# The blocks of w_out summed and split beside the last head's attention, and fetched as parts

## The chip, the cores and the metric

The kernel runs on one core of one Trainium2 chip. The metric is the time of one execution in microseconds (us), taken on the device; a kernel's time is the median of its runs. Times in profiles count from the start of the profiled execution's span, from its first to its last instruction.

## The reference

One layer of an encoder trunk, with SEQ = D_MODEL = 1024, in float32. What the change touches are the lines of the output projection; the rest is told as far as it stands around it.

```python
h = rmsnorm(x, norm_mix[l])
proj = h @ w_in[l]
q, k, v, r, lr_f, lr_b, u, g_a, g_b = jnp.split(proj, split_points, axis=-1)
...
o = o_fwd + o_bwd                       # gated linear attention, 4 heads, both directions
o = o * lax.rsqrt(jnp.mean(o * o, axis=-1, keepdims=True) + EPS)
o = (o * jax.nn.silu(r.astype(jnp.float32))).astype(x.dtype)
y_a = o @ w_branch_gla[l]
...
merged = jax.nn.sigmoid(g_a) * y_a + jax.nn.sigmoid(g_b) * y_b
x = x + merged @ w_out[l]
h2 = rmsnorm(x, norm_ffn[l])
gate, up = jnp.split(h2 @ w_ffn_in[l], 2, axis=-1)
x = x + (jax.nn.silu(gate) * up) @ w_ffn_out[l]
return rmsnorm(x, norm_final)
```

## The kernel before

**Products.** A float32 factor is split into a rounded part (`hi`, type float32r, a cast on ACT at L200) and the rest (`lo`, a subtraction at L201 on DVE or POOL); each product of two blocks is three matmuls, hi x hi, hi x lo and lo x hi (`mm3`, L279). The large products are also cut into 2 x 2 blocks and made by seven products of sums of blocks in place of eight (numbers p = 1 to 7 in the names). So sums of blocks of a weight are needed: for w_out those with p = 4, 5, 6 and 7; p = 1, 2, 3 take a block as it is. An output has its columns interleaved in two halves; `sorted_` reads a row sorted (elements two apart), `halves` reads it in natural order as two halves.

**Stages**, in order of time: norm, q, k, v and the attention of four heads, to about 310 us; the projection of R in six steps j = 0 to 5 of two halves, to about 342 (`feature_major`; what j = 0 to 2 give is put by, and from j = 3 on each half ends in two calls of `gated`, one for j - 3 that was put by and one for j: SiLU on ACT, four transposes `tp<-ident,ol` of the attention's output on PE, a product on DVE, L1206); the gates (gate n = 0 to 10), to about 554; the branch project with w_branch (14 pieces in the order p = 1, 2, 6, 5, 7, 3, 4, two each), to 629; the merged project with w_out (p = 1, 4, 6, 7, 5, 2, 3), to 709; then the FFN and the last norm.

**What sets the order.** The schedule is written out: every engine executes its instructions, and SP issues all DMAs, in the order in which the program emits them. `pump` (L161) is called after each product with the time that this product takes in units of a matmul of 512 columns; it lets work run that stands beside: `pending` (splits of the next weights), `side` (attention of the next head) and `aside`. `aside` holds jobs that `prepare_beside` (L735) put there; `beside` (L695) does one per `every` units: issue stores that are `put` steps old, subtract for the part `lo`, cast for the part `hi`, then the job's own sum. `finish_beside` (L738) runs what is left of them at once. In the projection of R this is called at the first half from j = 3 on at which no attention is left in `side`.

**The sums of w_out** (`output_jobs`, L629): for each of four rows k of blocks, two loads of 512 KB (`wsum`, L608), and four subtractions on POOL, each stored into `t_wo`, 256 KB. They are queued at gate n = 1 and run from 353 to 415 us. A merged piece with p = 4, 5, 6 or 7 loads two such sums (`wraw`, L1312) and splits them with two casts on ACT (L200) and two subtractions on POOL (L201).

**The last head's attention** runs from `side` beside the projections at about 260 to 310 us. Its state is a chain: a step on DVE (`st`, L924), two scalings on ACT (`sb`, `so`, L928 and L932), a step on DVE again. `raw` are the tiles of weights for the next projection and `ol` the attention outputs of a head that come back from HBM (`load_o`, L1040), one head at each of j = 2, 3 and 4. The transposes for j read the head j // 2: those of j = 4 read the third head, loaded at j = 4, ahead of its first half.

**Merging** (`merge`, L1625): the branch's block (1,1), made while p = 7 ends, adds a gate product `yb` on POOL (L1639) whose rows are read with `sorted_`.

Of the kernel before, what the change touches and what calls it, by code (L numbers as in the profile page):

```python
# [17 lines left out]
P = 128  # L18
# [35 lines left out]
def kernel(  # L54
# [537 lines left out]


    s_out = {p: dram.tile([P, 4, HALF], F32, name=f"s_out{p}") for p in (3, 5, 6, 7)}
    t_wo = {p: dram.tile([P, 4, HALF], F32, name=f"t_wo{p}") for p in (4, 5, 6, 7)}
    READY = 2
    f_order = [f for q in range(PAIRS) for f in (q, q + PAIRS)]
    u_out = [{p: dram.tile([P, 2, HALF], F32, name=f"u_out{n}_{p}") for p in range(1, 8)} for n in range(READY)]
# [31 lines left out]
    def output_jobs(k):  # L630
        (b11, b12, b21, b22), loads = rows_of(w_out, k)
        yield from loads
        for dst, a, b, p in ((b11, b12, b11, 5), (b12, b22, b12, 7), (b22, b22, b11, 6), (b21, b21, b22, 4)):
            yield partial(psub, dst, a, b), None, t_wo[p][:, k, :]

    def unit_jobs(n):
        raw = [slot(F32, (KT, P), "fraw")[:, :, :] for _ in range(2)]
# [54 lines left out]
            return [t2(dtype=F32R, s=s)[:, :] for s in ("uph", "upl")]  # L692
        return [slot(F32R, s=s)[:, :, :] for s in ("trh", "trl")]

    def beside(jobs, every, put, lag):  # L695

        casts, differ = [None] * lag, None
        puts = [[] for _ in range(put)]
        while True:
            job = next(jobs, None)  # L700
            if not any((job, *casts, differ, *puts)):
                return
            if put:
                for pair in puts.pop(0):
                    nc.sync.dma_start(*pair)
            puts.append([])
            if differ:
                src, (hi, lo), dst = differ
                nc.vector.tensor_tensor(lo, src, as_f32(hi), op=ALU.subtract)
                if len(src.shape) == 2:  # L710
                    puts[-1] += [(dst[:, i, :], as_f32(t)) for i, t in enumerate((hi, lo))]
                else:
                    right.setdefault(dst, []).append((hi, lo))
            differ, cast = None, casts.pop(0)
            if cast:
                src, dst = cast
                parts = parts_for(src)
                nc.scalar.copy(parts[0], src)
                differ = src, parts, dst
            casts.append(None)  # L720
            if job:
                op, src, dst = job
                if op:
                    op()
                if src is not None:
                    casts[-1] = src, dst
                elif dst is not None:

                    puts[-1].append((dst, op.args[0]))
            if not put:  # L730
                for pair in puts.pop():
                    nc.sync.dma_start(*pair)
            yield every

    def prepare_beside(jobs, every, put=PUT, lag=1):  # L735
        aside.append([beside(chain(*jobs), every, put, lag), every])

    def finish_beside():  # L738
        while aside:
# [329 lines left out]
    for h in range(HEADS):  # L1069
        if h:  # L1070
            project_qk(h, h == 2)
        else:
            first_qk()
            begin(attention(0))
        if h < HEADS - 1:
            begin(attention(h + 1))
        if h == 0:
            for ts in ((7,), (6,), (5, 4)):
                pair_products(ts)
            prepare_beside(map(branch_jobs, range(4)), 4.2)  # L1080
        if h == 2:
            value_weights.pop().products()

    class Unit:
# [206 lines left out]
    def line_load():  # L1291
        if len(loads) < len(line):
            loads.append(line[len(loads)][0]())

    def line_sums():
        if len(begun_sums) < len(line):
            begun_sums.append(line[len(begun_sums)][1]())

    def line_make():
        n = len(made)  # L1300
        if n < len(line):
            while len(loads) <= n:
                line_load()
            if len(begun_sums) <= n:
                while len(begun_sums) <= n:
                    line_sums()
                settle()
            made.append(line[n][2](loads[n]))

    def weight_load(src):  # L1310
        raw = slot(s="wraw")
        nc.sync.dma_start(raw[:, :, :], src)  # L1312
        return raw

    def weight_split(raw):
        parts = []
# [66 lines left out]
    def merged_piece(p, c):  # L1383
        def load():
            if p in WEIGHT_B:
                i, j = WEIGHT_B[p]
                return weight_load(chunk(w_out, i, j, c))
            return weight_load(t_wo[p][:, 2 * c : 2 * c + 2, :])

        def sums():  # L1390
            def block(i, j):
                return merged[i, j][c][:, :, :]

            if p == 6:
# [11 lines left out]
        return load, sums, make  # L1406

    line += [merged_piece(p, c) for p in MERGED for c in range(2)]

# [53 lines left out]
    class Gates:  # L1463
# [7 lines left out]
        def row(self, i):  # L1471
            while len(self.rows) <= i:
                self.rows.append(slot(s="ga"))
            return self.rows[i]

        def run(self, p):
            while len(right.get(p, ())) < 2:
                next(aside[0][0])
            ps = bank_of(self, p)
            product(self.unit, p, ps, right)  # L1480
            ps = ps[:, :]
            if self.kind in "ur":
                ps = sorted_(ps)
            finish_late()

            def row(i, half):
                t = self.row(i)[:, half, :]
                return halves(t) if self.kind in "ur" else t

            part = {1: (0, 0), 6: (0, 1), 5: (1, 1)}.get(p)  # L1490
            if part:
                nc.scalar.copy(row(*part), ps)  # L1492
                return
            i, half = {2: (0, 0), 3: (0, 1), 4: (1, 0), 7: (1, 1)}[p]
            done = row(i, half)
            if p != 4:
                add(done, ps, done)
# [16 lines left out]
        def pooling(self, i, half):  # L1514
            yb = bank(ps_g, "yb")
            mm3(
                yb[:, :], tuple(t[:, i * P : (i + 1) * P] for t in wpool[self.at]),
                tuple(t[:, half, :] for t in pools[self.at]), True, True,
            )
            j, row = 2 * self.at + i, self.row(i)[:, half, :]  # L1520
            late.append(partial(
                nc.vector.scalar_tensor_tensor, row, yb[:, :], g_pool[:, j : j + 1], row, op0=ALU.mult, op1=ALU.mult
            ))

        def store(self, i):
# [58 lines left out]
    def project(base, products, collect, before, amid=None, first=FIRST, up=UP, pools_of=lambda p: U_BANKS if p == 1 else X_BANKS):  # L1584
        banks = {}
        for at, p in enumerate(products):
# [4 lines left out]
            for c in range(2):  # L1591
# [36 lines left out]
    def merge(i, j, m, ps, s):  # L1628
# [6 lines left out]
        if (i, j) == (1, 1):  # L1635
            dst = halves(dst)
            add(dst, sorted_(ps), sorted_(s))
            nc.vector.tensor_tensor(dst, dst, sorted_(sa), op=ALU.mult)
            padd(dst, dst, sorted_(yb))  # L1639
            return  # L1640
        if s is not None:
            add(ps, ps, s)
# [513 lines left out]
```

## Time and profile before

| | |
|---|---|
| median of 3 runs | 1325.27 us (1325.08 to 1325.62) |
| the profiled execution's own time | 1323.53 us |
| its span | 1321.8 us |
| attention and projections, 0 to 310 us | PE busy 303.82 us |
| projection of R, 310 to 342 | PE busy 32.00 of 32.00 us |
| gates, 342 to 554 | PE busy 211.32 of 212.00 us |
| branch project, 554.57 to 629.45 | PE busy 73.11 of 74.88 us |
| merged project, 629.67 to 709 | PE busy 77.05 of 79.33 us |
| FFN and end, 709 to 1321.8 | PE busy 604.08 of 612.80 us |

The rows by stage are busy times of TensorE (PE) in stretches of the span. PEld is its loading of weights, DVE is VectorE, ACT is ScalarE, POOL is GpSimd, SP is SyncE, which issues DMAs. A row of the timeline gives start and duration in us, engine, line, operation, output<-inputs, shapes and count, and in brackets the idle time ahead and what ended it. A row of a tile gives the durations in ns (least/median/most) and the first and last start. A row of a wait gives the total, the number of times and the longest. A row of windows gives for each engine busy time and instructions, then the granted clock of PE (1.00 is full), the DMA engines' share and GB/s.

### The profile page before, as it was taken

What the parts mean: (1) busy time and instruction counts of PE and PEld (TensorE: products, weight loads), DVE (VectorE), ACT (ScalarE), POOL (GpSimd) and SP (SyncE); (2) the same over time, 40 slices, a digit from 0 to 9 for tenths busy, and PEclk for the clock granted to TensorE, in tenths of its full rate; (3) what the DMA queues carried; (4) which work ended last, traced back from release to release, by engine and by line L of the source; (5) the groups of instructions that cost most, each with busy time, mean ns of one, the idle gap of its engine ahead of it and who ended that gap; (6) DMA issues with size and microseconds to landing.
All of it is one profiled execution on the core that took longest, in us unless ns stands there. A gap on an engine that the chain in (4) does not pass through costs nothing. (4 is left out here: it accounts for less than half of the span.)

```text
span 1321.8 us, 17901 instructions
## 1 busy us (share of the span) xinstructions
PE 1302.2 (99%) x6310; PEld 1138.0 (86%) x6310; DVE 838.3 (63%) x1034; ACT 645.3 (49%) x1177; POOL 769.0 (58%) x557
## 2 busy tenths in 40 slices
PE   9999999999999999999999999999999999999998
PEld 7888888899888888888888888888888888888886
DVE  6975556554735876778884856566666657354375
ACT  7366766665534545554347633333333334454353
POOL 3332734132598657669675286777766778465454
PEclk9999999999999999999999999999999999999999
DMA  7231623134778678996516355555444457995562
GB/s 236 104 104 42 198 75 117 59 101 128 239 247 283 195 223 303 380 409 212 185 65 240 127 189 186 183 183 173 155 142 159 150 160 257 382 349 201 182 223 80
DMA packets 167835, 251.97 MB, mean 191 GB/s; under 512 B 11161, under 2 KB 94145, under 8 KB 167745
## 3 DMA queue, kind: packets, MB, share of 16 engines
q1 hardware_dynamic: 167600, 250.57, 55.8%
q8 instruction: 49, 0.80, 0.3%
q14 instruction: 42, 0.34, 0.1%
q10 hardware_dynamic: 144, 0.26, 0.1%
HBM read 168.74 MB, written 82.05 MB: 190 GB/s over the span
## 5 line engine op out<-in xcount | busy, mean ns | idle before, releaser
L201 POOL TENSOR_TENSOR wl<-fs,wh 128x512 fp32r<-128x512 f32 x124 | 190.7, 1543 | 138.8 <-ACT wh L200 80.9
L279 PE MATMUL ps<-gh,wh 128*128 128x512 f32 x616 | 234.4, 381 | 0.5 <-DVE sums L1880 0.3
L279 PE MATMUL ps<-gl,wh 128*128 128x512 f32 x616 | 233.6, 379 | 0.7 <-DVE gl L1713 0.7
L279 PE MATMUL ps<-gh,wl 128*128 128x512 f32 x616 | 233.5, 379 | 0.0
L201 POOL TENSOR_TENSOR wl<-fraw,wh 128x512 fp32r<-128x512 f32 x93 | 131.1, 1410 | 58.0 <-ACT wh L200 52.8
L201 POOL TENSOR_TENSOR ol<-gor,oh 128x1024 fp32r<-128x1024 f32 (+1 forms) x42 | 103.2, 2462 | 76.0 <-ACT oh L200 63.1
L279 PE MATMUL ps<-hh,wh 128*128 128x512 f32 x356 | 141.1, 396 | 0.7 <-ACT ga L1492 0.7
L279 PE MATMUL ps<-hh,wl 128*128 128x512 f32 x356 | 134.9, 379 | 0.0
L279 PE MATMUL ps<-hl,wh 128*128 128x512 f32 x356 | 134.9, 379 | 0.0
L279 PEld LDWEIGHTS ps<-gh,wh 128*128 128x128 f32 x616 | 116.5, 189 | 17.9 <-DVE sums L1880 0.7
L279 PEld LDWEIGHTS ps<-gl,wh 128*128 128x128 f32 x616 | 116.4, 189 | 17.4 <-DVE gl L1713 1.1
L279 PEld LDWEIGHTS ps<-gh,wl 128*128 128x128 f32 x616 | 116.4, 189 | 16.5
L279 PE MATMUL ps<-oh,oh 128*128 128x512 f32 x308 | 116.8, 379 | 0.2 <-DVE g L1886 0.2
L279 PE MATMUL ps<-ol,oh 128*128 128x512 f32 x308 | 116.7, 379 | 0.0
L279 PE MATMUL ps<-oh,ol 128*128 128x512 f32 x308 | 116.7, 379 | 0.0
L201 POOL TENSOR_TENSOR wl<-wraw,wh 128x512 fp32r<-128x512 f32 x56 | 91.4, 1663 | 38.3 <-ACT wh L200 36.2
L201 POOL TENSOR_TENSOR wl<-raw,wh 128x512 fp32r<-128x512 f32 x34 | 47.0, 1392 | 103.2 <-ACT wh L200 70.3
L201 DVE TENSOR_TENSOR ol<-wor,oh 128x1024 fp32r<-128x1024 f32 (+1 forms) x42 | 66.6, 1601 | 62.6 <-ACT oh L200 55.1
L200 ACT CAST wh<-fs 128x512 fp32r<-128x512 f32 x124 | 75.8, 612 | 25.7 <-DVE fs L1104 23.8
L279 PEld LDWEIGHTS ps<-hh,wl 128*128 128x128 f32 x356 | 67.3, 189 | 9.6
L279 PEld LDWEIGHTS ps<-hh,wh 128*128 128x128 f32 x356 | 67.4, 189 | 9.3 <-ACT ga L1492 1.1
L279 PEld LDWEIGHTS ps<-hl,wh 128*128 128x128 f32 x356 | 67.4, 189 | 8.4
(281 smaller groups left out, 3059.4 us busy)
## 6 DMA issues: line engine op xcount, KB each, us to landing
fraw<-in_w_ffn_in_dram SPq DMA_DIRECT2D x44, 512.0 KB, 5.9
gor<-g_out SPq DMA_DIRECT2D x35, 512.0 KB, 5.7
fraw<-in_w_in_dram SPq DMA_DIRECT2D x22, 512.0 KB, 6.1
g_out<-s SPq DMA_DIRECT2D x44, 256.0 KB, 2.4
wor<-t_out SPq DMA_DIRECT2D x20, 512.0 KB, 4.2
raw<-in_w_in_dram SPq DMA_DIRECT2D x36, 256.0 KB, 5.2
g_out<-g SPq DMA_DIRECT2D x33, 256.0 KB, 2.6
x<-in_x_dram SPq DMA_DIRECT2D x16, 512.0 KB, 5.2
```

The lines of the kernel that those rows point to most:

```text
L200: nc.scalar.copy(hi, src)
L201: eng.tensor_tensor(lo, src, as_f32(hi), op=ALU.subtract)
L279: nc.tensor.matmul(ps.rearrange("p (c a) -> p c a", a=2), a, b.rearrange("p (a c) -> p c a", a=2), **flags)
```

## The change

Three parts. (1) `output_jobs` moves from gate n = 1 (`every` 2.8, `put` 3, `lag` 1) to the third head's turn in the loop over heads (h = 2, `every` 3.3, `put` 1, `lag` 2, first job after 32 units), beside the last head's attention. The sums are now also split there, by a cast on ACT and a subtraction on DVE for each of 16, and `t_wo` holds both parts, so that a store has 512 KB. (2) The merged pieces with p = 4, 5, 6, 7 fetch both parts straight into the tiles `wh` and `wl`: 32 loads of 256 KB in place of 8 loads of 512 KB, 16 casts on ACT and 16 subtractions on POOL. (3) The gate product that the branch's block (1,1) adds (`yb`, gates of kind "b", half 0, `at` >= 2) is written with its rows sorted, so that `merge` reads them in natural order.

```diff
-    t_wo = {p: dram.tile([P, 4, HALF], F32, name=f"t_wo{p}") for p in (4, 5, 6, 7)}
+    t_wo = {p: dram.tile([P, 4, 2, HALF], F32, name=f"t_wo{p}") for p in (4, 5, 6, 7)}
...
-            yield partial(psub, dst, a, b), None, t_wo[p][:, k, :]
+            yield partial(psub, dst, a, b), dst, t_wo[p][:, k]
...
-    def beside(jobs, every, put, lag):
+    def slot_parts(src):
+        w = slot(F32R, s="wop")
+        return w[:, 0, :], w[:, 1, :], w[:, :, :]
+
+    def beside(jobs, every, put, lag, home):
...
-                src, (hi, lo), dst = differ
+                src, (hi, lo, *both), dst = differ
                 nc.vector.tensor_tensor(lo, src, as_f32(hi), op=ALU.subtract)
-                if len(src.shape) == 2:
+                if both:
+                    puts[-1].append((dst, as_f32(both[0])))
+                elif len(src.shape) == 2:
...
-                parts = parts_for(src)
+                parts = home(src)
...
-    def prepare_beside(jobs, every, put=PUT, lag=1):
-        aside.append([beside(chain(*jobs), every, put, lag), every])
+    def prepare_beside(jobs, every, put=PUT, lag=1, home=parts_for, delay=None):
+        aside.append([beside(chain(*jobs), every, put, lag, home), every if delay is None else delay])
...
         if h == 2:
+            prepare_beside(map(output_jobs, range(4)), 3.3, 1, 2, slot_parts, 32)
             value_weights.pop().products()
...
+    fetched = {}
+
+    def line_fetch():
+        n = len(made)
+        if n < len(line) and n not in fetched and line[n][3:]:
+            fetched[n] = line[n][3]()
...
-            made.append(line[n][2](loads[n]))
+            line_fetch()
+            made.append(line[n][2](fetched.get(n) or loads[n]))
...
+    def weight_parts(src):
+        parts = [wts.tile([P, HALF], F32R, tag=s, name=name(s))[:, :] for s in ("wh", "wl")]
+        for i, t in enumerate(parts):
+            nc.sync.dma_start(as_f32(t), src[:, i, :])
+        return parts
...
-            return weight_load(t_wo[p][:, 2 * c : 2 * c + 2, :])
...
-            return data_split(a, 3.5 if p == 3 else 2), weight_split(raw)
+            return data_split(a, 3.5 if p == 3 else 2), weight_split(raw) if p in WEIGHT_B else raw
...
+        def fetch():
+            return [weight_parts(t_wo[p][:, 2 * c + k]) for k in range(2)]
...
+        def sorts(self, half):
+            return self.kind in "ur" or self.kind == "b" and half == 0 and self.at >= 2
...
-            if self.kind in "ur":
-                ps = sorted_(ps)
...
+            if self.sorts(half):
+                ps = sorted_(ps)
...
-            j, row = 2 * self.at + i, self.row(i)[:, half, :]
+            j, row, yb = 2 * self.at + i, self.row(i)[:, half, :], yb[:, :]
+            if self.sorts(half):
+                row, yb = halves(row), sorted_(yb)
...
-        if n == 1:
-            prepare_beside(map(output_jobs, range(4)), 2.8)
...
                 line_make()
+                line_fetch()
                 line_sums()
...
-            padd(dst, dst, sorted_(yb))
+            padd(dst, dst, halves(yb))
```

How the instructions stand on their engines shows what moves. First SP, in the kernel before, in the projection of R at j = 3 to 5. `raw` are weights of R (the first pair of j = 4, the second of j = 5), `hs` a sum for the gates, `ol` the third head's output, which `gated` reads at j = 4.

```order
L208 DMA raw_3155<-in_w_in_dram 128x4x128
L208 DMA raw_3157<-in_w_in_dram 128x4x128
L684 DMA hs_3349<-f_out_563 128x1024
L1044 DMA ol_3376<-o_out_567 128x1024
L1044 DMA ol_3377<-o_out_567 128x1024
L208 DMA raw_3380<-in_w_in_dram 128x4x128
L208 DMA raw_3382<-in_w_in_dram 128x4x128
```

The same place on SP in the changed kernel; `wop` is a sum of w_out in its two parts, `wsum` a row of w_out's blocks, and the stores to `t_wo` are of 512 KB.

```order
L709 DMA t_wo_544<-wop_3387 128x1024
L608 DMA wsum_3394<-in_w_out_dram 128x1024
L608 DMA wsum_3395<-in_w_out_dram 128x1024
L709 DMA t_wo_546<-wop_3391 128x1024
L709 DMA t_wo_545<-wop_3398 128x1024
L709 DMA t_wo_543<-wop_3404 128x1024
L709 DMA t_wo_544<-wop_3411 128x1024
L709 DMA t_wo_546<-wop_3415 128x1024
L709 DMA t_wo_545<-wop_3420 128x1024
L709 DMA t_wo_543<-wop_3424 128x1024
L684 DMA hs_3445<-f_out_563 128x1024
L1050 DMA ol_3472<-o_out_567 128x1024
```

Between the weights of j = 4 and `hs` now stand sixteen more DMAs, of which the last ten are shown: the stores wait for the parts, and the two loads of the last row stand behind a store.

DVE at the same place, in the kernel before: the products of `gated` in j = 3's first half (two rows), in its second half (two rows), and the first of j = 4.

```order
L1206 SCALAR_TENSOR_TENSOR o_3320<-tp_3315,cols,sr_3313 128x512
L1206 SCALAR_TENSOR_TENSOR o_3330<-tp_3325,cols,sr_3323 128x512
L1206 SCALAR_TENSOR_TENSOR o_3321<-tp_3362,cols,sr_3360 128x512
L1206 SCALAR_TENSOR_TENSOR o_3331<-tp_3370,cols,sr_3368 128x512
L1206 SCALAR_TENSOR_TENSOR o_3320<-tp_3430,cols,sr_3428 128x512
```

And in the changed kernel, from the second product of j = 3's first half on:

```order
L1213 SCALAR_TENSOR_TENSOR o_3375<-tp_3370,cols,sr_3368 128x512
L713 TENSOR_TENSOR wop_3333<-wsum_2957,wop_3333 128x512
L713 TENSOR_TENSOR wop_3380<-wsum_2957,wop_3380 128x512
L713 TENSOR_TENSOR wop_3387<-wsum_3329,wop_3387 128x512
L713 TENSOR_TENSOR wop_3391<-wsum_3329,wop_3391 128x512
L713 TENSOR_TENSOR wop_3398<-wsum_3330,wop_3398 128x512
L713 TENSOR_TENSOR wop_3404<-wsum_3330,wop_3404 128x512
L713 TENSOR_TENSOR wop_3411<-wsum_3394,wop_3411 128x512
L713 TENSOR_TENSOR wop_3415<-wsum_3394,wop_3415 128x512
L713 TENSOR_TENSOR wop_3420<-wsum_3395,wop_3420 128x512
L713 TENSOR_TENSOR wop_3424<-wsum_3395,wop_3424 128x512
L1213 SCALAR_TENSOR_TENSOR o_3366<-tp_3458,cols,sr_3456 128x512
```

Ten subtractions stand in a row between the two halves of j = 3.

The third place is SP beside the last head's attention. In the kernel before (`o_out` are stores of a head's output, the first `raw` are weights of R for j = 2, the second for j = 3):

```order
L574 DMA o_out_567<-o_2494 128x1024
L208 DMA raw_2832<-in_w_in_dram 128x4x128
L208 DMA raw_2834<-in_w_in_dram 128x4x128
L1044 DMA ol_2961<-o_out_565 128x1024
L1044 DMA ol_2962<-o_out_565 128x1024
L208 DMA raw_2965<-in_w_in_dram 128x4x128
```

In the changed kernel:

```order
L608 DMA wsum_2785<-in_w_out_dram 128x1024
L608 DMA wsum_2786<-in_w_out_dram 128x1024
L208 DMA raw_2836<-in_w_in_dram 128x4x128
L208 DMA raw_2838<-in_w_in_dram 128x4x128
L709 DMA t_wo_544<-wop_2894 128x1024
L608 DMA wsum_2956<-in_w_out_dram 128x1024
L608 DMA wsum_2957<-in_w_out_dram 128x1024
L1050 DMA ol_2982<-o_out_565 128x1024
L1050 DMA ol_2983<-o_out_565 128x1024
L208 DMA raw_2986<-in_w_in_dram 128x4x128
```

A store that waits for a sum's two parts, and the loads of the second row, stand ahead of `ol` and of the weights for j = 3.

More of the change, by code (lines that the diff above doesn't have):

```diff
@@ L1403, in make @@
             a = s3s[c] if p == 7 else merged[{1: (0, 0), 6: (0, 0), 5: (1, 0), 4: (1, 1), 2: (0, 1), 3: (0, 1)}[p]][c]
-            return data_split(a, 3.5 if p == 3 else 2), weight_split(raw)
-        return load, sums, make
+            return data_split(a, 3.5 if p == 3 else 2), weight_split(raw) if p in WEIGHT_B else raw
+        def fetch():
+            return [weight_parts(t_wo[p][:, 2 * c + k]) for k in range(2)]
+        return (load, sums, make) if p in WEIGHT_B else (load, sums, make, fetch)
     line += [merged_piece(p, c) for p in MERGED for c in range(2)]
@@ L1487, in row @@
                 t = self.row(i)[:, half, :]
-                return halves(t) if self.kind in "ur" else t
+                return halves(t) if self.sorts(half) else t
             part = {1: (0, 0), 6: (0, 1), 5: (1, 1)}.get(p)
+            i, half = part or {2: (0, 0), 3: (0, 1), 4: (1, 0), 7: (1, 1)}[p]
+            if self.sorts(half):
+                ps = sorted_(ps)
             if part:
@@ L1493, in run @@
                 return
-            i, half = {2: (0, 0), 3: (0, 1), 4: (1, 0), 7: (1, 1)}[p]
             done = row(i, half)
@@ L1519, in pooling @@
             )
-            j, row = 2 * self.at + i, self.row(i)[:, half, :]
+            j, row, yb = 2 * self.at + i, self.row(i)[:, half, :], yb[:, :]
+            if self.sorts(half):
+                row, yb = halves(row), sorted_(yb)
             late.append(partial(
-                nc.vector.scalar_tensor_tensor, row, yb[:, :], g_pool[:, j : j + 1], row, op0=ALU.mult, op1=ALU.mult
+                nc.vector.scalar_tensor_tensor, row, yb, g_pool[:, j : j + 1], row, op0=ALU.mult, op1=ALU.mult
             ))
```

## The prediction

> **What bounds the kernel now.** I read the page's busy times first, then PE's lists of waits, then rows of the timeline at the places that the change touches.
>
> ```profile
> span 1321.8 us, 17901 instructions
> PE 1302.2 (99%) x6310; PEld 1138.0 (86%) x6310; DVE 838.3 (63%) x1034; ACT 645.3 (49%) x1177; POOL 769.0 (58%) x557
> PE ps L279 <- POOL wl L201: 2.7, 4, 1.4
> PE ps L279 <- ACT ga L1492: 0.7, 1, 0.7
> ```
>
> PE is busy 99% of the span. The last two rows are lists of waits, of 560 to 760 us (2.7 us in four waits for parts of weights, in the two stages whose weights change) and of the gates, 342 to 554 us: one wait, and not for the sums of w_out that are made there. Since PE executes the same instructions in the same order in both kernels, the time can change only by what PE waits for and by its clock. The profiled execution took 1323.53 us, 1.73 above its span; the runs' median, 1325.27, is 1.74 above the profiled execution. I sum on 1323.53 and add 1.74 at the end.
>
> **What goes.** Two of the four waits, and the row of PE ahead of one:
>
> ```profile
> 655.73 0.48 PE L279 MATMUL ps<-wh,dh 128*128 128x512 f32 x1
> 657.60 0.48 PE L279 MATMUL ps<-wl,dh 128*128 128x512 f32 x1 [1.39 <-POOL wl L201]
> ...
> 619.05 0.48 PE L279 MATMUL ps<-dh,wl 128*128 128x512 f32 x1 [0.62 <-POOL wl L201]
> ...
> 319.94 0.38 PE L279 MATMUL ps<-hl,wh 128*128 128x512 f32 x1
> 322.75 0.38 PE L279 MATMUL ps<-hh,wl 128*128 128x512 f32 x1
> 322.96 1.04 PE L1199 MATMUL tp<-ident,ol 128*128 128x128 f32 x8
> ```
>
> From 319.94 to 322.75 stand 14 matmuls, so one starts every 2.81 / 13 = 0.216 us. From 655.73 to 657.60 are 1.87 us, so this wait cost 1.65, not its 1.39 of idle time: with some 0.2 more for each, the four cost 2.7 + 4 x 0.2 = 3.5 us. The wait at 657.60 (merged piece p=6) is for a subtraction `wl` that the change drops, since both parts come from HBM. The one at 619.05 (branch piece p=4) is late because POOL is held up:
>
> ```profile
> 607.54 10.22 POOL L1639 TENSOR_TENSOR mg<-mg,gate 128x512 f32<-128x512 f32 x4
> 617.72 10.92 POOL L201 TENSOR_TENSOR wl<-wraw,wh 128x512 fp32r<-128x512 f32 x8
> ...
> L724 POOL TENSOR_TENSOR wsum<-wsum x16: 1263/1280/1751, 111.7 to 413.7; 128x512 f32<-128x512 f32 x16
> L200 ACT CAST wh<-wraw x56: 608/618/625, 548.8 to 696.2; 128x512 fp32r<-128x512 f32 x56
> L201 POOL TENSOR_TENSOR wl<-wraw,wh x56: 1264/1291/2873, 549.5 to 698.7; 128x512 fp32r<-128x512 f32 x56
> ```
>
> The four additions with rows sorted take 10.22 us; an operation of this size in natural order has a median of 1.28 (row `wsum`), so they would take 5.1, and `wl` is ready some 5 us earlier, against 0.62 us of wait. The 16 dropped casts and 16 dropped subtractions (0.62 and 1.29 each) are otherwise beside PE's work and worth nothing. The 32 loads of parts are beside it too: a piece is 24 matmuls, 24 x 0.216 = 5.2 us, and with six buffers of parts a load can be issued when the piece three back has ended, 10.4 us ahead, against a landing of 4.7 in the median and 8.8 at most (row below). If one were as late as that and queued too, it would cost about 2. I take **-3.5**, with -4 and -2 as ends. In the gates nothing is gained, as PE doesn't wait there for what leaves.
>
> **What comes: the burst in the projection of R.** The order of the changed kernel shows that the sums of w_out are not through when the last head ends. At j=3, second half, the rest is flushed: ten subtractions in a row on DVE, nine casts on ACT, eight sums on POOL, and SP's stores, among which stand the loads of the last rows of w_out. Behind them on SP stand `hs`, `ol_3472` and the weights of j=5. PE's second group of transposes after j=4's first half reads `ol_3472`; in the row above these eight start at 322.96, the second four at about 323.2.
>
> ```profile
> 315.40 1.41 DVE L1206 SCALAR_TENSOR_TENSOR o<-tp,cols,sr 128x512 f32<-128x512 f32 x2
> 277.49 0.68 DVE L201 TENSOR_TENSOR kt<-kp,kt 128x512 fp32r<-128x512 f32 x1
> ...
> L705 SPq DMA_DIRECT2D t_wo<-wsum x16: 319/352/2657, 372.6 to 415.0; - x16
> L608 SPq DMA_DIRECT2D wsum<-in_w_out_dram x8: 333/452/999, 353.7 to 398.9; - x8
> DMA to landing us min/median/max: 2.8/5.5/6.7
> ...
> DMA to landing us min/median/max: 2.8/4.7/8.8
> ...
> L1044 SPq DMA_DIRECT2D ol<-o_out x6: 338/402/495, 260.7 to 302.3; - x6
> DMA to landing us min/median/max: 4.0/4.0/4.0
> ...
> 301.87 0.81 SPq L1044 DMA_DIRECT2D ol<-o_out  x2
> 302.78 0.94 SPq L208 DMA_DIRECT2D raw<-in_w_in_dram  x2
> ```
>
> The landings are, in turn, of the tiles `wsum`, `t_wo` and `ol`. SP issued `ol` at 301.87, 21 us ahead of its use. Now, at the old times:
> - DVE is through with j=3's first half at 315.40 + 1.41 = 316.8. Three subtractions of 0.68, up to `wop_3387`, end at 318.85.
> - Only then does SP issue that store (0.35) and the two loads of the last rows (0.45 each), from 319.2 and 319.65; they land 5.5 later, 325.15.
> - Four sums in series on POOL, 4 x 1.28: 330.3. A cast on ACT, 0.62: 330.9. The last subtraction, 0.68: 331.6.
> - SP issues the last store and `hs` (0.35 each), then `ol_3472` from 332.3; landing 4.0 later: 336.3.
>
> PE would stand from 323.2 to 336.3, **13.1 us**. Ends: loads that land in 2.8 give 10.4; loads of 6.7, POOL at 1.75 each and a landing of `ol` behind 1 MB of stores (at the 410 GB/s of the row in the next part, 2.5 us) give 13.1 + 1.2 + 1.9 + 2.5 = 18.7. As DVE subtracts while POOL adds, I put POOL midway (+0.9) and take **+14**, range 10 to 18.7. Next behind come the weights of j=5, issued at 333.1; with the 5.2 below, a cast and a subtraction of POOL's they are there at 340.2, and PE, which takes 6.06 us for a half (316.91 to 322.96 between transposes), needs them at about 343: hidden.
>
> The Trainium skill (GPSIMD Engine Reference, 1. Specifications) says that GpSimd shares its SBUF interfaces with VectorE and contends with instructions of two SBUF inputs, as these subtractions are; by it all four sums run slow, and the term would be 15.0 rather than 14.0. The spread 1263 to 1751 of the row `wsum` agrees that some do; it doesn't show with what.
>
> **What comes: the last head.** SP's load of R's weights for j=3, `raw_2986`, issued at 264.02, now stands behind the store of the first split sum.
>
> ```profile
> 264.02 1.62 SPq L208 DMA_DIRECT2D raw<-in_w_in_dram  x2
> 283.89 0.60 ACT L200 CAST wh<-raw 128x512 fp32r<-128x512 f32 x1
> 290.54 0.69 DVE L201 TENSOR_TENSOR p<-sc,p 128x512 fp32r<-128x512 f32 x1 [0.93 <-ACT p L200]
> 291.93 0.28 PE L279 MATMUL op<-vh,p 128*128 128x256 f32 x1
> ...
> raw<-in_w_in_dram SPq DMA_DIRECT2D x36, 256.0 KB, 5.2
> ...
> 560.00:580.00 20.00, 20.00 (x94) 17.53 (x93) 14.58 (x12) 9.92 (x16) 12.75 (x8) 1.00 1.03 410
> ```
>
> That store needs DVE's `wop_2894`, which takes the place of `kt` at 277.49 and ends at 278.2. SP then issues it, two loads of `wsum`, two of `ol` and `raw`: 0.35 + 2 x 0.45 + 2 x 0.4 = 2.1, so `raw` at 280.3, landing at 285.5, or at 288 if 3 MB ahead of it move at the 410 GB/s that the last row shows (3 MB / 410 = 7.3 us). Its cast stood at 283.89, inside ACT's chain of states, so that chain shifts by 1.6 to 4.1; an added cast (0.62) and an added subtraction (0.68) follow on the way to `p`. `p` was ready at 291.23, 0.7 ahead of PE's use of its second part at 291.93. The stall is 1.6 + 1.3 - 0.7 = 2.2 to 4.7; I take **+4**, since much is in flight together, and 1 to 6 as bounds, for a cover that I overlooked or a later step of the same chain.
>
> **The clock.** PE's last matmul starts at 1315.12:
>
> ```profile
> 1315.12 0.38 PE L279 MATMUL ps<-oh,ol 128*128 128x512 f32 x1
> 1317.00:1319.00 2.00, 0.00 (x0) 0.00 (x0) 0.75 (x1) 0.72 (x1) 0.15 (x1) 1.00 0.23 88
> 1319.00:1321.80 2.80, 0.00 (x0) 0.00 (x0) 0.00 (x0) 0.00 (x0) 0.00 (x0) 0.70 0.42 160
> ```
>
> The granted clock is 1.00 until 1319 and 0.70 in the 2.8 us behind. At half speed 0.70 is 1.12 us full and 1.68 half, so it fell at 1320.1, 4.6 us after PE came to rest. A stall of 14 us outlasts that. How long it stays low after work returns no row shows: nothing at one end, as long as the fall took at the other, 4.6 us at half speed, which costs 2.3. I take **+1.5**, nearer the end that a row gives. The Trainium skill (TensorE: Matmul & The Clock Gate, Part 1: The HAM clock gate) has one idle window of about 3.4 us for the drop and as much busy time for the return; by it, as an estimate, 1.7.
>
> **Sum.** 1323.53 - 3.5 + 14 + 4 + 1.5 = 1339.5; with 1.74, **1341.3 us**. My own case spans -4 + 10 + 1 + 0 = +7 (1332) to -2 + 18.7 + 6 + 2.3 = +25 (1350.3).
>
> **Rivals.**
> - *No stall: the loads are in time* (faster). Only the 3.5 go: 1321.8. The point is whether `ol_3472` is issued before 319.2, 4.0 ahead of its use. It would be if the jobs were through before the last head's end. Against: DVE reaches the burst only at 316.8, and a load, four sums, a cast and a subtraction still have to follow. 5%.
> - *The burst bites short* (slower, little). If the last rows' loads, sums and casts ran during the last head, only stores stood ahead of `ol`: DVE's ten subtractions, 316.8 + 6.8 = 323.6, then 0.7 of issues and a landing of 4.0 give 328.3, a stall of 5.1; with 1 to 4 in the attention and -3.5: 1328 to 1331. Against: SP's order has those loads behind `wop_3387`. 10%.
> - *The burst bites longer.* All of DVE's and POOL's work contended, stores of 512 KB ahead of every load, and `p`'s delay at its upper bound: +18 to +22 and +6, so 1348 to 1352. For it: `wl` above reaches 2873 ns, over twice its median. 12%.
> - *The parts don't cure the later waits*: loads in six buffers come late and cost what the subtractions did; 1341.3 + 3.5 = 1344.8, inside my range. 10%.
>
> **Chances.** My forecast 63%, the last rival 10 within its range, short 10, long 12, no stall 5. The range 1332 to 1350.5 leaves out the short burst, the fast case and a part of the long. Faster by over 0.2% (2.65 us, about what a measurement of this kernel can tell from no change) 0.05, same 0.04, slower 0.91.
>
> **What would show it.** In the changed profile: PE idle some 14 us before the second transposes of j=4, released by the DMA of `ol`, with the granted clock below 1 behind; SP's `ol` issued near 336 (with the shift of 4) rather than 302; PE idle some 4 us before `op<-vh,p`; no wait for `wl` between 650 and 665 nor at 619. I am wrong if SP issues `ol` before the burst ends, if PE does other work in that gap, or if the jobs come out earlier in the last head than the row order lets me place them.

## The result and the profile after

The changed kernel takes 1357.98 us (median of 4 runs, 1357.29 to 1360.53) against 1325.17: 1.0249 of the time before, 95% interval 1.0236 to 1.0262. It is slower by 32.8 us, where I had forecast 16; the time lies above my range. The profiled execution is the run of 1360.53 us, 2.6 us above the median, so its terms add up to 37.0 us (1358.8 against 1321.8 of span) and not to 32.8.

The page of the changed kernel, and PE's list of waits:

```profile
span 1358.8 us, 17913 instructions
PE 1308.0 (96%) x6310; PEld 1141.8 (84%) x6310; DVE 848.8 (62%) x1050; ACT 645.6 (48%) x1177; POOL 738.5 (54%) x541
PE tp L1206 <- DMA ol<-o_out: 23.9, 1, 23.9
PE op L279 <- ACT p L200: 6.0, 3, 5.2
PE ps L279 <- ACT ga L1519: 2.3, 2, 1.6
PE ps L279 <- POOL wl L201: 1.7, 2, 0.9
...
PE ps L279 <- DVE dl L165: 1.3, 1, 1.3
```

Both waits stand where the prediction put them: for the third head's `ol` at j=4, and for `p` in the last head. Since PE's order is the same, the same instruction of PE can be set beside itself, and the difference of its start times shows where time was lost:

| PE's instruction | before | after | difference | grown by |
|---|---|---|---|---|
| last one ahead of `op<-vh,p` | 291.49 | 293.59 | 2.1 | +2.1 (1.5 in small waits of the last head's states; 0.6 stood there at 156 us, before anything that the change moves) |
| `op<-vh,p` | 291.71 | 299.21 | 7.5 | +5.4 (wait for `p`) |
| last one ahead of `tp<-ident,ol` | 323.29 | 334.09 | 10.8 | +3.3 (low clock) |
| `tp<-ident,ol` | 323.40 | 358.30 | 34.9 | +24.1 (wait for `ol`) |
| last one ahead of `ps<-trh,wh` in the gates | 346.97 | 384.41 | 37.4 | +2.5 (low clock) |
| `ps<-trh,wh` | 347.19 | 386.37 | 39.2 | +1.8 (wait for `ga`) |
| late in the FFN | 1313.17 | 1350.08 | 36.9 | -2.3 (branch and merged project) |

The windows of the changed kernel show the clock (PEclk is the third column from the end):

```profile
293.00:299.00 6.00, 0.97 (x5) 0.51 (x3) 3.14 (x5) 3.83 (x8) 5.11 (x5) 0.96 0.30 119
299.00:301.00 2.00, 1.79 (x7) 1.56 (x8) 0.69 (x1) 0.68 (x2) 0.67 (x1) 0.50 0.99 223
...
305.00:307.00 2.00, 2.00 (x12) 1.79 (x11) 0.86 (x2) 0.47 (x2) 0.00 (x0) 0.91 0.07 22
...
336.00:340.00 4.00, 0.00 (x0) 0.00 (x0) 0.00 (x0) 0.00 (x0) 0.00 (x0) 0.94 0.98 282
350.00:358.00 8.00, 0.00 (x0) 0.00 (x0) 0.45 (x1) 0.00 (x0) 0.00 (x0) 0.50 0.97 294
360.00:364.00 4.00, 4.00 (x12) 3.21 (x11) 0.52 (x1) 3.20 (x5) 2.50 (x2) 0.57 1.08 287
```

It falls to half in both waits, at 298.5 (0.96 of 6 us) and at 339.5 (0.94 of 4 us). A share of 0.91 in 305 to 307 is 0.36 us at half speed, so after the first wait it stays low until 305.4, 6.2 us from PE's start at 299.21; 0.57 in 360 to 364 gives 363.4, 5.1 us from 358.30.

The burst itself, by DVE's, POOL's, SP's and PE's rows:

```profile
324.30 6.51 DVE L1036 TENSOR_SCALAR o<-o,ors 128x256 f32<-128x256 f32 x8 [1.75 <-POOL ors L316]
330.74 1.39 DVE L1213 SCALAR_TENSOR_TENSOR o<-tp,cols,sr 128x512 f32<-128x512 f32 x2
332.06 3.68 DVE L713 TENSOR_TENSOR wop<-wsum,wop 128x512 fp32r<-128x512 f32 x6
...
325.85 2.67 POOL L730 TENSOR_TENSOR wsum<-wsum,wsum 128x512 f32<-128x512 f32 x2 [0.24 <-DMA wsum<-in_w_out_dram]
...
340.98 1.26 POOL L730 TENSOR_TENSOR wsum<-wsum 128x512 f32<-128x512 f32 x1 [11.10 <-DMA wsum<-in_w_out_dram]
342.96 3.12 POOL L730 TENSOR_TENSOR wsum<-wsum,wsum 128x512 f32<-128x512 f32 x2 [0.71 <-DMA wsum<-in_w_out_dram]
346.16 1.59 POOL L730 TENSOR_TENSOR wsum<-wsum 128x512 f32<-128x512 f32 x1
...
334.53 2.38 SPq L608 DMA_DIRECT2D wsum<-in_w_out_dram  x2
350.06 1.63 SPq L1050 DMA_DIRECT2D ol<-o_out  x2
...
358.30 1.09 PE L1206 MATMUL tp<-ident,ol 128*128 128x128 f32 x4 [23.95 <-DMA ol<-o_out]
```

The reader is to follow one chain down these rows: DVE reaches the burst at 332.1, SP issues the loads of the last row from 334.53, POOL has the second load at 342.96 and its four sums at 347.75, SP issues `ol` at 350.06, and PE goes on at 358.30.

### The profile page after: what moved, and what is told of

Its sections match the earlier page's. It is cut to its first block, busy times and chain, and to the rows that moved or that the text cites. A ratio compares the mean times of both kernels' runs of the same rounds, so it can differ in the third digit from the quotient of the medians.

```text
span 1358.8 us, 17913 instructions
## 1 busy us (share of the span) xinstructions
PE 1308.0 (96%) x6310; PEld 1141.8 (84%) x6310; DVE 848.8 (62%) x1050; ACT 645.6 (48%) x1177; POOL 738.5 (54%) x541
## 5 line engine op out<-in xcount | busy, mean ns | idle before, releaser
L201 POOL TENSOR_TENSOR wl<-fs,wh 128x512 fp32r<-128x512 f32 x124 | 187.5, 1517 | 160.0 <-ACT wh L200 101.0
L201 POOL TENSOR_TENSOR wl<-wraw,wh 128x512 fp32r<-128x512 f32 x40 | 65.9, 1677 | 49.9 <-ACT wh L200 27.8
L200 ACT CAST wh<-fs 128x512 fp32r<-128x512 f32 x124 | 75.9, 613 | 25.6 <-DVE fs L1111 23.9
```

Of the source, the lines that this page charges most:

```text
L200: nc.scalar.copy(hi, src)
L201: eng.tensor_tensor(lo, src, as_f32(hi), op=ALU.subtract)
```

## The experiments

The first figure is a kernel's median; its ratio is to runs of the kernel before on the same chip.

### What is left at j=3, and the order of SP

**half_moved.** Only rows 0 and 1 stay beside the last head.

```diff
-            prepare_beside(map(output_jobs, range(4)), 3.3, 1, 2, slot_parts, 32)
+            prepare_beside(map(output_jobs, range(2)), 3.3, 1, 2, slot_parts, 32)
...
+        if n == 1:
+            prepare_beside(map(output_jobs, range(2, 4)), 2.8, 1, 1, slot_parts)
```

> Only the first two rows of w_out's sums stay beside the last head; the other two are summed and split beside the gates. SP then has no loads behind the burst's stores, and 2 subtractions instead of 10 stand in it. Theory A (the burst at j=3 costs the time: SP's `ol` behind loads, sums and stores): the wait for `ol` of 23.9 us is under 3, its clock loss (4.3) goes too, the wait before the last head's `p` (5.2 + 2.6 of clock) stays: 1328 to 1333 us. Rival B (the work itself costs the time wherever it stands beside PE): half of it at the same place keeps half of the loss, 1340 to 1346.

1340.86 us, ratio 1.0118 (1.0099 to 1.0138). PE's waits between 280 and 370 us:

```profile
PE op L279 <- ACT p L200: 5.2, 1, 5.2
PE tp L1206 <- DMA ol<-o_out: 4.3, 1, 4.3
PE ps L279 <- ACT ga L1519: 3.5, 1, 3.5
```

Half of the work takes the wait for `ol` from 23.9 to 4.3: it is not in proportion to the work beside the last head. But it isn't under 3, and the time lies at the lower edge of rival B's. What theory A had left out are two stores ahead of `ol`, which lands 8.3 us after its issue, and the start of the gates behind it, where PE waits 3.5 us for `ga`.

**half_put3.** The same with each store issued two steps later.

```diff
-            prepare_beside(map(output_jobs, range(2)), 3.3, 1, 2, slot_parts, 32)
+            prepare_beside(map(output_jobs, range(2)), 3.3, 3, 2, slot_parts, 32)
```

> As half_moved, with stores issued three steps after their sums instead of one, so that SP's load of R's weights for j=3 stands ahead of the first store instead of behind it. Theory A2 (the wait before `p` is made by that load, which ACT's cast inside the chain of states waits for): the wait falls from 5.2 to under 1.5 and no clock is lost there: 4 to 8 us under half_moved, 1323 to 1326. Rival B2 (it is the added casts, subtractions and sums that lengthen the chain): the same as half_moved within 1.5.

1335.58 us, ratio 1.0076 (1.0058 to 1.0094): 5.3 under half_moved. PE's wait for `p` in 280 to 360 us, and DVE's scaling of the last head's output:

```profile
PE op L279 <- ACT p L200: 1.6, 1, 1.6
...
317.30 2.19 DVE L1036 TENSOR_SCALAR o<-o,ors 128x256 f32<-128x256 f32 x8 [1.75 <-POOL ors L316]
```

The wait for `p` falls from 5.2 to 1.6 by the order on SP alone: most of it was the load of R's weights for j=3, not the added instructions. It is not quite the "under 1.5" of theory A2, and the time lies above the range given, as half_moved's did. In the changed kernel's rows that load is issued at 283.63 and ACT's cast, inside the chain of states, waits for it until 291.45:

```profile
283.63 1.57 SPq L208 DMA_DIRECT2D raw<-in_w_in_dram  x2
...
291.45 0.62 ACT L200 CAST wh<-raw 128x512 fp32r<-128x512 f32 x1 [3.10 <-DMA raw<-in_w_in_dram]
```

**ol_early.** The changed kernel, `ol` for j=4 loaded at j=3.

```diff
-        if 2 <= j <= 4:
+        if 2 <= j <= 3:
             load_o(j - 2)
+        if j == 3:
+            load_o(2)
```

> The changed kernel, with the third head's `ol` loaded one step of j earlier, ahead of the burst on SP; nothing else. Theory A (SP's order behind the burst): PE no longer waits for `ol`, but runs 6 us on and then waits for the weights of j=5, which stay behind the burst: a wait of 15 to 20, and 1352 to 1357 us. Rival D (only `ol` is late, by its long landing behind the stores): the wait goes as a whole, 1329 to 1334.

1351.76 us, ratio 1.0197 (1.0175 to 1.0219), 6.2 under the changed kernel. PE's waits between 280 and 370:

```profile
PE tp L1206 <- DVE o L1213: 9.2, 1, 9.2
PE ps L279 <- ACT wh L200: 6.0, 1, 6.0
```

The 23.9 us become 9.2 + 6.0. The wait goes to two others behind the same burst, one of them not expected: PE's next transposes need the banks that DVE reads with its two products behind the ten subtractions. Then come the weights of j=5, as expected. Rival D falls; the time is theory A's, at the lower edge of its range.

**three_rows.** Rows 0 to 2 beside the last head (as half_moved, with `range(3)` and `range(3, 4)`).

> Three rows of w_out's sums stay beside the last head, the fourth is made beside the gates. At j=3 six subtractions and their stores are still run in one go, but no load, sum or cast of a new row stands between them. Theory A (the serial chain load, sums, cast, subtraction inside the burst is most of the 23.9 us): `ol` is issued when DVE's six subtractions are through, near 337, and lands 4 to 8 later; PE waits 7 to 11 for it, 1341 to 1348 us. Rival B (the burst costs by its number of subtractions and stores): 6 of 10 remain, a wait of 14 to 15, and 1348 to 1352.

1349.12 us, ratio 1.0174 (1.0159 to 1.0189). PE waits 13.4 us for `ol`; its row, then SP's and DVE's:

```profile
PE tp L1206 <- DMA ol<-o_out: 13.4, 1, 13.4
...
321.23 16.77 SPq L709 DMA_DIRECT2D t_wo<-wop  x7
338.09 1.15 SPq L684 DMA_DIRECT2D hs<-f_out  x1
339.33 1.70 SPq L1050 DMA_DIRECT2D ol<-o_out  x2
...
324.11 6.54 DVE L1036 TENSOR_SCALAR o<-o,ors 128x256 f32<-128x256 f32 x8 [1.75 <-POOL ors L316]
331.89 3.69 DVE L713 TENSOR_TENSOR wop<-wsum,wop 128x512 fp32r<-128x512 f32 x6
```

So the fourth row with its serial chain is worth 10.5 of the 23.9 us, less than half; theory A's size falls, and the time is B's. With 2, 6 and 10 subtractions left at j=3 (half_moved, this kernel, the changed one) the wait is 4.3, 13.4 and 23.9: near proportion to what is left there. DVE's six subtractions end at 335.6 here, but `ol` is issued at 339.33 and PE goes on at 347.59: 3.7 us of issues and 8.3 of landing, without any wait for a sum. That left three suspects: DVE's scaling (6.54 us where it took 2.19), SP's issues of 1.15 us, and the landing.

**dense.** All rows, earlier and at shorter steps, so that none is left at j=3.

```diff
-            prepare_beside(map(output_jobs, range(4)), 3.3, 1, 2, slot_parts, 32)
+            prepare_beside(map(output_jobs, range(4)), 1.6, 1, 2, slot_parts, 4)
```

> All four rows beside the last head, but begun after 4 units instead of 32 and a step every 1.6 instead of 3.3, so that no job is left at j=3. Theory A (only what is left at j=3 makes the wait for `ol`): that wait is gone; SP's stores and loads now stand ahead of the weights for j=2 and j=3, so the waits of the last head grow to 8 to 15 us: 1335 to 1345. Rival E (beside the last head there is no room for this work on any engine): the last head is longer by over 25 us, above 1350.

1348.21 us, ratio 1.0171 (1.0153 to 1.0188). PE's waits between 250 and 342:

```profile
PE kp L916 <- DVE ke L898: 9.9, 2, 8.8
PE kv L279 <- ACT kt L200: 5.2, 1, 5.2
PE op L279 <- ACT p L200: 3.0, 1, 3.0
PE kv L279 <- DVE kt L201: 2.1, 1, 2.1
```

The wait for `ol` is gone, as A says, but the last head waits 20 us instead. Both sizes were missed: the time lies between the two theories. Beside the last head there is room for part of this work only.

### The suspects by themselves

**pool_beside.** The kernel before, with four subtractions of a scratch tile on POOL.

```diff
         if h == HEADS - 1:
+            d = t2(s="dum")
+            nc.gpsimd.memset(d[:, :], 0.0)
+            for _ in range(4):
+                psub(d[:, :], d[:, :], d[:, :])
             unscaled.pop()()
```

> The kernel before with four subtractions of a scratch tile added on POOL, 128x512 each, at the place where the changed kernel's POOL makes w_out's sums beside DVE's scaling of the last head's output (eight operations of 128x256, 2.19 us in the profile before, 6.51 in the changed one). Theory G (POOL's two-input operations slow DVE's scaling): it takes 5 to 7 us here, POOL's four 5.1 to 7, and the time stays within 0.2% as PE has 20 us to spare there. Rival H (DMA traffic or something else of the burst slows DVE): it stays at 2.2.

1326.06 us, ratio 1.0010 (0.9999 to 1.0021). DVE's and POOL's rows:

```profile
313.75 7.98 DVE L1030 TENSOR_SCALAR o<-o,ors 128x256 f32<-128x256 f32 x8 [1.75 <-POOL ors L316]
...
314.27 4.40 POOL L1040 TENSOR_TENSOR dum<-dum 128x512 f32<-128x512 f32 x4
318.75 2.57 POOL L201 TENSOR_TENSOR wl<-raw,wh 128x512 fp32r<-128x512 f32 x2
```

DVE's eight scalings take 7.98 us in place of 2.19, as long as POOL goes on (to 321.3), with no added transfer. POOL is not slowed: its two `wl` take 1.28 each. Theory G is shown; the rise was more than expected, as POOL's next two subtractions stand there too.

**behind_stores, behind_stores2.** The kernel before, with three stores of 512 KB ahead of `ol` for j=4; in the second, between its two loads.

```diff
         for half in range(2):
+            if h == 2 and half:
+                spare = dram.tile([3, P, 4, DV], F32, name="spare")
+                for n in range(3):
+                    nc.sync.dma_start(spare[n], o_heads[1][0][:, :, :])
             nc.sync.dma_start(o_heads[h][half][:, :, :], o_out[h][:, 4 * half : 4 * half + 4, :])
```

> The kernel before with three stores of 512 KB, of a tile that is long there, put on SP ahead of the load of `ol` for j=4; nothing else. Theory J (the load's 8.2 us in the changed kernel, against 4.0 in the profile before, and SP's 1.15 us for an issue against 0.35, come from transfers in flight ahead of and beside it): the fourth DMA in a row takes 1.1 us to issue and `ol` lands 6.5 to 8.5 after its issue; no wait on PE, as there are 20 us to spare, and the time stays within 0.2%. Rival K (they come from waits of SP or from the attention's output itself): issues at 0.35, landing 4 to 5.

1325.58 us, ratio 1.0004 (0.9994 to 1.0014). It could not tell: SP issued the stores near 289, and `ol` had to wait for its tile until 301.83. But it gives the load's duration in its usual company, with no store just ahead: its second half lands after 5.1 us, and not the 4.0 of the profile before.

> As behind_stores, but the three stores stand between the two loads of `ol` for j=4, so that SP reaches them only when the first load has its tile, near 302 us. Theory J: from the fourth DMA in a row on an issue takes 1.1 us, and the second load of `ol` lands 6.5 to 8.5 after its issue. Rival K: issues of 0.35, landing 4 to 5. The time within 0.2% either way, as that load is needed at 329.

1327.26 us in its one run, beside 1323.15 to 1326.39 before; no more can be said of the time. SP's rows, and the landings of `ol` in this kernel:

```profile
303.01 2.14 SPq L1047 DMA_DIRECT2D spare<-ol  x3
305.25 1.49 SPq L1048 DMA_DIRECT2D ol<-o_out  x1
306.84 1.97 SPq L208 DMA_DIRECT2D raw<-in_w_in_dram  x2
...
DMA to landing us min/median/max: 4.2/5.8/7.5
...
L1047 SPq DMA_DIRECT2D spare<-ol x3: 383/423/1230, 303.0 to 303.9; - x3
```

The fourth and fifth DMA in a row take 1.23 and 1.49 us to issue, and the fifth, the load behind the stores, lands after 7.5, in a kernel that makes no sum there. So theory J holds and rival K falls: stores just ahead are enough for both in its profile. That the issue itself waits for the transfers in flight is an inference: 512 KB in 1.15 to 1.25 us would be 420 to 455 GB/s, about the most that the window of 560 to 580 us showed (410).

### The gates, and what the parts bring

**natural_only.** The kernel before with part 3 of the change.

> The kernel before with part 3 of the change alone: the gate product written with its rows sorted, so that POOL adds it in natural order. My prediction's step (the wait at branch piece p=4 goes): 1.3 us, 1324.0. By the start times in the changed kernel's profile only 0.4 of it goes: 1324.8. Rival (nothing): 1325.2.

1325.64 us, ratio 1.0000 (0.9990 to 1.0010): nothing. POOL's additions and the subtractions behind them:

```profile
608.07 7.82 POOL L1644 TENSOR_TENSOR mg<-mg,gate 128x512 f32<-128x512 f32 x4
615.85 11.93 POOL L201 TENSOR_TENSOR wl<-wraw,wh 128x512 fp32r<-128x512 f32 x8
```

The four additions take 7.82 us in place of 10.22, not the 5.1 that I had, and the eight subtractions behind them 11.93 in place of 10.92, so POOL is through only 0.9 us earlier.

**gates_parts.** The sums made and split beside the gates; parts 2 and 3 stay.

```diff
-            prepare_beside(map(output_jobs, range(4)), 3.3, 1, 2, slot_parts, 32)
...
+        if n == 1:
+            prepare_beside(map(output_jobs, range(4)), 2.8, 1, 1, slot_parts)
```

> The sums are made and split beside the gates, where before made them, and everything else of the change stays (parts fetched, rows in natural order). Theory A: no wait is added, what the change removes in the later stages is kept: 2.1 by the difference of start times of PE from the gates to the FFN between the two profiles, so 1322.5 to 1324 us. Rival C (splits beside the gates or loads of parts cost what they save): 1325 to 1328.

1330.97 us, ratio 1.0040 (1.0026 to 1.0054): worse than theory A and rival C both. ACT's row at the largest wait of its gates:

```profile
412.51 0.59 ACT L1518 COPY ga<-ps 128x512 f32<-128x512 f32 x1 [5.58 <-DMA t_wo<-wop]
```

A copy of a gate waits 5.58 us for a large tile that a store still holds; there are 39 such tiles.

**gates_t2, and other steps.** The parts go into small tiles (the line above without `slot_parts`); then `every` 2.0, 2.4 and 3.6 in place of 2.8.

> As gates_parts, but the two parts go into small tiles of the pool of intermediate results instead of the 39 large ones. Theory F (the 5.8 us that gates_parts lost came from large tiles held until their store had landed, for which ACT's copies of the gates waited): that wait goes, 1322.5 to 1325 us. Rival C (the added casts and subtractions in the gates' order make it): 1328 to 1332.

> As gates_t2 with a step every 2.0 units instead of 2.8, so that the sums are through before the pooling begins to use the same small tiles. Theory F2 (what gates_t2 still loses, 2.6 us, comes from the last row's parts meeting the pooling's start): 1322.5 to 1325 us. Rival C (any place beside the gates costs 2 to 3 us): 1327 to 1331.

> As gates_t2_20 with a step every 2.4 units. F2: between the two, 1323 to 1327. Rival C: 1327 to 1331.

> As gates_t2 with a step every 3.6 units: thinner, but longer beside the pooling. F2: worse than gates_t2's 1328.3, 1329 to 1333. Rival I (density counts, not the pooling): better, 1324 to 1327.

| kernel | median, us | ratio (95% interval) |
|---|---|---|
| gates_t2 (2.8) | 1328.30 | 1.0023 (1.0013 to 1.0033) |
| gates_t2_20 | 1330.45 | 1.0044 (1.0031 to 1.0056) |
| gates_t2_24 | 1328.55 | 1.0030 (1.0018 to 1.0043) |
| gates_t2_36 | 1340.38 | 1.0118 (1.0104 to 1.0132) |

Small tiles bring about half of what gates_parts lost (2.6 us instead of 5.8), so theory F is half of it, and the time is rival C's. F2 falls at steps of 2.0 and 2.4: an earlier end is no better, and the kernel loses 5.4 and 3.5 us. At 3.6 it loses 15, more than F2 said: two waits for `ga` take 12.8 us, and rival I falls. What makes the loss at the shorter steps was not tried any further; it stays open.

**p6_slot, p6_t2, p6_sorted.** Of the sixteen sums only the four for p=6 are split and fetched as parts; made at gate n=1 with `every` 2.8, `put` 3, `lag` 1 as before, in large tiles, in small ones, and in large ones without part 3.

```diff
-            yield partial(psub, dst, a, b), dst, t_wo[p][:, k]
+            yield partial(psub, dst, a, b), dst if p == 6 else None, t_wo[p][:, k]
...
+            if p != 6:
+                return weight_load(t_wo[p][:, 2 * c : 2 * c + 2, :])
...
-        return (load, sums, make) if p in WEIGHT_B else (load, sums, make, fetch)
+        return (load, sums, make) if p != 6 else (load, sums, make, fetch)
```

> The sums are made beside the gates as in the kernel before (every 2.8, put 3, lag 1); only those for p=6 are split there (4 casts and subtractions instead of 16) and fetched as parts, into large tiles; rows in natural order as in the change. Theory L (what the parts bring is the wait of the merged piece p=6, 2.1 us, and what they cost grows with the number of splits in the gates): 1322.5 to 1324.5 us. Rival M (the gates have no room for any split): 1325.5 to 1328.

> As p6_slot with the parts in small tiles. Theory L: the same within 0.5 us. If large tiles held until their store lands are what the gates lack: 0.5 to 2 us better than p6_slot.

> As p6_slot without part 3: the gate product in natural rows, added by POOL with its rows sorted, as in the kernel before. If part 3 brings nothing here either, as in natural_only: 1320.8 to 1322 us, the same as p6_slot. If the merged pieces need POOL early: 0.5 to 1.5 us slower than p6_slot.

| kernel | median, us | ratio (95% interval) |
|---|---|---|
| p6_slot | 1321.29 | 0.9974 (0.9963 to 0.9985) |
| p6_t2 | 1321.67 | 0.9969 (0.9957 to 0.9980) |
| p6_sorted | 1322.33 | 0.9981 (0.9972 to 0.9990) |

All three are faster than the kernel before, by 2.6 to 4.3 us of their medians. PE's waits of p6_slot from 342 to 554 us, and the one for `wl` from 560 to 760:

```profile
PE ps L279 <- ACT ga L1520: 0.7, 1, 0.7
...
PE ps L279 <- POOL wl L201: 0.8, 1, 0.8
```

The gates have the one wait that they had before, and the waits for `wl` fall from 2.7 to 0.8 us. So theory L's mechanism holds: four splits fit beside the gates, sixteen don't. Its size was too small, as p6_slot lies below L's range of 1322.5 to 1324.5: a wait for `dl` of 0.8 us in the branch project, which L had not counted, is gone as well. p6_t2 is no better than p6_slot, so the hold of four stores on large tiles costs nothing that shows here. The intervals of the three overlap; whether part 3 adds anything stays open.

## Why the prediction was wrong

- **Direction, places and order: right.** Slower, with PE waiting for `ol` behind the burst and for `p` behind a load that stood behind a store. The rivals "no stall" and "the burst bites short" fell; "the burst bites longer" had the right sign and too little (1348 to 1352).
- **The burst: the term of 14 us measured 24.1**, and this is the step that failed first. The path was right, and durations on it were wrong. "DVE is through with j=3's first half at 315.40 + 1.41 = 316.8", moved by 10.8, would be 327.6; DVE was through at 332.1. Its scaling of the last head's output, which stands ahead, took 6.51 us instead of 2.19 since POOL made sums beside it (shown by pool_beside and half_put3): 4.3 of these 4.5. And "landing 4.0 later" came from a row in which least, median and most are the same, a single load in a quiet queue; it took 8.2 (350.06 to 358.30). SP issued the loads of the last row 1.2 us apart instead of 0.45, and the second was used from 342.96, 8.4 us after the first issue, where I had 5.95. By behind_stores2 that is what transfers just ahead do; 1.1 of the 4.2 belongs to the load's usual company (5.1 in behind_stores). 4.5 + 4.2 + 2.5 = 11.2 are the 11.0 between the plain sum of 13.1 and 24.1. The 0.9 that I put on POOL was there (its three sums behind the second load took 4.79 us, and 3 x 1.28 are 3.84), but the first of the four had been made ahead of that load (340.98), so from there to the issue of `ol` it took 7.1 us, as in my sum.
- **POOL and DVE.** The Trainium skill (GPSIMD Engine Reference, 1. Specifications) names the contention of the shared interfaces. The traces agree, and show who pays. Of the eight scalings in the changed kernel four took 1.37 to 1.46 us, and each of these ends 0.15 us behind one of POOL's four sums; the other four took 0.34. POOL's sums stayed at 1.28 to 1.31, so DVE alone paid. Between DVE's subtractions and POOL's sums both did:

```profile
320.07 1.31 DVE L713 TENSOR_TENSOR wop<-wsum,wop 128x512 fp32r<-128x512 f32 x1
...
319.56 1.28 POOL L201 TENSOR_TENSOR wl<-raw,wh 128x512 fp32r<-128x512 f32 x1 [3.07 <-ACT wh L200]
320.80 1.72 POOL L730 TENSOR_TENSOR wsum<-wsum 128x512 f32<-128x512 f32 x1
```

DVE's subtraction, 0.68 us elsewhere, begins inside POOL's first operation and ends 0.54 after it; POOL's next, 1.28 elsewhere, begins inside DVE's and ends 1.14 after it.

- **The last head: 4 us measured 6.9**, 5.4 in the wait for `p` and 1.5 in small waits ahead of it that I had not priced. The mechanism was right (half_put3 took the wait to 1.6 by the order on SP). SP issued `raw` at 283.63, not 280.3: the subtraction that its store waits for began at 279.70, not 277.49, and took 1.20 us, not 0.68. The cast began 7.8 us after the issue of `raw`, not 5.2, with a store and four loads of 512 KB issued just ahead.
- **The clock: 1.5 measured 5.8**, 3.3 and 2.5. I charged one drop; the wait for `p` of 5.2 us was enough for another. After each, it stayed low 6.2 and 5.1 us from the first matmul on, longer than my upper end of 4.6. It is also longer than the about 3.4 us of busy time that the Trainium skill (TensorE: Matmul & The Clock Gate, Part 1: The HAM clock gate) gives as the least. The clock changed at 298.5, 305.4, 339.5 and 363.4 us: 6.9, 34.1 and 23.9 apart, which is 2, 10 and 7 times 3.41 within 0.1. So it seems to change only at steps of 3.4 us, and a wait's cost then depends on where in a step it ends; no run tested that.
- **"Hidden" behind the burst: 1.8 us were not.** I followed the weights of j=5, which came in time, but not the loads of `hs` behind them. PE waits for a copy of ACT, `ga`, at the gates' first product with `trh`, and in 360 to 390 us ACT's casts of `trh` wait for `hs`, as its list of waits shows; that the one makes the other wasn't tried.

```profile
ACT trh L724 <- DMA hs<-f_out: 6.6, 3, 3.1
```

- **The saving: 3.5 measured 2.3.** The waits of piece p=6 went, worth 2.35 by start times. Of the two of piece p=4 the first went (0.9) and the second grew (by 0.5), in the changed kernel as in natural_only: the rows' order was not what made POOL's additions slow. The quickest takes 1.91 us with sorted rows and 1.89 in natural order; of the 10.22 us before, one addition alone took 4.19, and why is not known. A wait for `dl` in the branch project grew by 0.7, so part 3 bought nothing in sum.

## What to carry to other kernels

Before work is moved beside a stage, follow in the new order what is left of it when that stage ends: on every engine and on the issue of DMAs the rest stands ahead of all that follows, and moving only the load that PE waited for (ol_early) gave back 6 of 33 us. A duration from a quiet place is a lower end; ask what runs beside it after the change, and take a row of the same operation in company. Split ahead of time only what TensorE waits for: four splits for one piece won 2.6 to 4.3 us, sixteen lost 2.6 to 33, by where they stood.

## What the runs showed that I had not expected

- Two-input operations on POOL stretched DVE's eight 128x256 scalings from 2.19 to 7.98 us, while POOL's own stayed at their usual length; beside DVE's subtractions of two inputs, POOL's took up to 1.78 us instead of 1.28.
- From about the fourth DMA of 512 KB in a row an issue took 1.1 to 1.5 us instead of 0.35, and a load behind three stores landed after 7.5 instead of 5.1.
- A wait of 5.2 us cost another 3.3 us by the clock, and one of 24 only 2.5: in these two, the cost did not grow with the length of the wait.
